# Retention heads of a FoX/RetNet trunk: the second head's p2 product moved up to p1 and p5, and a PSUM bank for each half of the first head's queries and keys

## Chip, cores and metric

The kernel runs on one core of one Trainium2 chip. The metric is the device time of one execution in microseconds (us), lower is better; the time shown is the median of three runs.

## The reference, cut to what matters

Two layers on a sequence of 512 rows of width 2048, all in float32: a forgetting-attention layer, then a chunkwise retention layer with 8 heads. The change lies in the retention layer, whose projections and heads are these:

```
proj = jnp.einsum('bsd,de->bse', x, w_in)
q, k, v, gate = jnp.split(proj, [...], axis=-1)
q = rotary(q.reshape(B, S, RET_HEADS, RET_QK_DIM))
k = rotary(k.reshape(B, S, RET_HEADS, RET_QK_DIM)) * (RET_QK_DIM ** -0.5)
...
inner = jnp.einsum('bhqd,bhkd->bhqk', qc, kc) * intra_decay[None]
...
o = group_norm_heads(o).reshape(B, S, RET_V_WIDTH)
y = o * jax.nn.silu(gate)
return jnp.einsum('bse,ed->bsd', y, w_out)
```

A head's queries and keys are 256 columns each, its values and gates 512 each.

## The kernel before, in words

**Products.** Every projection is a matrix product of 2x2 quarters. A `Unit` does it in Strassen's way with seven products p1 to p7 of sums of quarters; a `Plain` unit does the eight plain products. Each float32 operand is split into a high and a low part (`split`: ScalarE writes the high part w_h, L305, then VectorE subtracts to the low part w_l, L306), and each product is three matmuls (L310, L311, L312). A product is cut into blocks along the contraction: a wide unit (values and gates, 512 columns) has four blocks a product with 12 matmuls of 512 columns each, a narrow unit (queries and keys) two with 24 of 256. A `Unit` adds into three accumulators, x, y and z, each a tile of two PSUM banks (the kernel calls such a tile a bank, and so does this text; tags b0, b1, b2, kept in the list `banks`). p1, p6, p7 and p4 add into x, p2 into y, p5 and p3 into z. When a product ends whose sum is needed later, ScalarE copies its accumulator to SBUF (`keep`, L423) into a buffer with one of the tags k0, k1, k2, y0.

**Order of blocks.** `ORDER` lists the products in groups whose blocks alternate: p1 with p5 (one block later), then p6, then p3 with p7, then p2 with p4. A pair in `SHARES` (p2 before p4) that stands side by side shares one loaded quarter of the weights. Buffers for loaded quarters are few: three tags and a fourth, `room`; chains of sums sit in four w_q buffers; there are three pairs of w_h and w_l.

**Retention layer.** Head 0's queries and keys are a `Plain` unit run in two halves, `EACH[0]` (rows m = 0) and `EACH[1]` (m = 1). Between the halves head 0's wide unit does p2 and p1 (`FIRST`), and after them p5, p6, p3, p7 and p4 (`REST`). Both halves of queries and keys use one bank, `banks[0]`; ScalarE copies a half out of it (`take_qk`, L1576, tile qk_raw). `REST`'s p5 then uses that same bank as its z. Heads 1 to 7 each do a narrow unit and then a wide unit in `ORDER`.

**What else runs.** A planner (`Order`) writes the program: it places a block of matmuls a slot, and between blocks the steps of tasks, as far as rings of buffers are free and the work handed to VectorE and ScalarE stays under a limit. If a block or a `keep` needs a buffer that is not free, `require` places steps of waiting tasks one after another, with no block between them, until it is. Two tasks run beside a head's wide unit. `attend` does the rotary embedding of the head's own queries and keys on VectorE (tile rope, L1609 to L1616), splits them (qk_h, qk_l), and does four scores (mmp<-qk_h), a mask (L1659) and a split (inner). `retain` ends the head before: bn_stats, a Newton inverse root in small VectorE steps (L289 to L301, L1733), four times a scaling on ScalarE (L1753), a transpose on TensorE (L1740), two copies (y L1744, ny L1745), and stores issued on POOL. At its third step `retain` gives back the buffer k0 (first gate half), which the wide unit's p1 is to be kept in. Head 1's p5 is kept in y0, the other heads' in k1.

Of the kernel before, what the change touches and what calls it, by code (L numbers as in the profile page):

```python
# [23 lines left out]
RH = 8  # L24
# [28 lines left out]
FIRST = (("p2",), ("p1",))  # L53
REST = (("p5",), ("p6",), ("p3", "p7"), ("p4",))
ORDER = (("p1", "+p5"), ("p6",), ("p3", "p7"), ("p2", "p4"))

EARLY = (("p1",), ("p5",), ("p2", "p6"), ("p3",), ("p7",), ("p4",))

# [29 lines left out]
class Order:  # L88
# [29 lines left out]
    def spawn(self, steps, rank=2):  # L118

        task = dict(steps=steps, last=self.now - 1, rank=rank)  # L120
        try:
            task["need"] = next(steps)
        except StopIteration:
            return
        at = sum(t["rank"] <= rank for t in self.tasks)
        self.tasks.insert(at, task)
# [104 lines left out]
def trunk(ctx: ExitStack, tc: tile.TileContext, xq, x, fb_f, columns, wf_in, narrow, wide, ln_g, ln_b, rot, decay,  # L231
# [94 lines left out]
    banks = ["b0", "b1", "b2"]  # L326
# [37 lines left out]
    class Unit:  # L364
# [3 lines left out]
        def __init__(self, w, n, sink, rows=True, u2="k0", p1="k0"):  # L368
            self.w, self.n, self.sink, self.rows, self.u2, self.p1 = w, n, sink, rows, u2, p1
            self.wide = w is wide  # L370
            self.shape = [P, 2, 512] if self.wide else [P, 4, 256]
            self.blocks = 8 // self.shape[1]
            self.tags = None
            self.early = self.between = self.adds = False
            self.p15_tag = self.p5 = "k1"
            self.bank, self.kept, self.chain, self.lent, self.summed = {}, {}, {}, {}, {}
            self.left = {p: self.blocks for p in FORM}
            self.kept_w, self.of = {}, {}
# [115 lines left out]

        def run(self, order=ORDER, then={}, leaves=False, last=False):


            self.early = order is EARLY
            self.leaves, self.last = leaves, last
            order = blocks_of(self.blocks, *order)  # L500

            i = order.index(("p3", self.blocks - 1)) if ("p3", 0) in order else 0
            if order[i + 1:i + 3] == [("p7", self.blocks - 1), ("p4", 0)]:
                order[i:i + 2] = order[i + 1], order[i]
            for i, (p, c) in enumerate(order):
                shares = i + 1 < len(order) and order[i + 1] == (SHARES.get(p), c)
                shared = i > 0 and order[i - 1] == ({"p7": "p3", "p4": "p2"}.get(p), c)
                turned = p == "p7" and order[i + 1] == ("p3", c) or p == "p3" and order[i - 1] == ("p7", c)
                e = (0,) if last and p == "p4" else (0, 1)
                o.push(Block(self, p, c, e, shares, shared, then.get(i), then.get(p), turned))  # L510
            for c in range(4 if last else 0):
                o.push(Block(self, "p4", c, (1,), False, False, None, None))
# [362 lines left out]
    def fetch_while(i):  # L875

        take = lambda *names: lambda: spawn(fetch_forms(i, names))
        return {"p5": take("a11"), "p6": take("s1"), "p7": take("s2", "s4"), "p4": take("s3", "a12", "a22")}
# [632 lines left out]
    def biases():  # L1511

        nc.gpsimd.dma_start(row_b, ln_b[1:2, :])
        for s in range(8):
            yield need(wait=12)
            nc.gpsimd.dma_start(out[s * 64:(s + 1) * 64, :], row_b[0:1, :].to_broadcast([64, D]))
# [23 lines left out]
    class Head:  # L1540
        def __init__(self, h):
            self.h = h
            self.raw = self.v = None
            self.ends = [], []
            self.have = self.have_v = self.have_g = 0
            self.gates = {}
            self.attended = False
            if h == 0:
                self.qk_unit = Plain(narrow, 8, self.take_qk, lambda: [banks[0]] * 2, rows=False)
            else:  # L1550
                self.qk_unit = Unit(narrow, 8 + h, self.take_qk, rows=False, u2="y0")
                if h == 1:

                    self.qk_unit.u2, self.qk_unit.p15_tag = "k1", "y0"
            self.vg_unit = Unit(wide, 6 + h, self.take_vg, u2="k2")
            if h == 1:
                self.vg_unit.p5 = "y0"

        def take_qk(self, m, n, tile, done):

# [223 lines left out]
    for h in heads[1:]:  # L1784
        if h.h == 2:
            spawn(biases())
        h.qk_unit.run(then={"p3": lambda h=h: spawn(h.attend())})
        then = fetch_while(1) if h.h == RH - 1 else {}
        last = then.get("p4", lambda: None)
        h.vg_unit.run(leaves=h.h == RH - 1,  # L1790
                      then={**then, "p4": lambda h=h, last=last: (spawn(h.retain()), last())})


# [141 lines left out]
```

## Time and profile before

| | before |
|---|---|
| median of 3 runs | 2405.23 us (2400.59 to 2405.72) |
| the profiled execution | 2403.45 us |
| its span, first to last instruction | 2401.7 us |
| mean granted TensorE clock | 0.988 |
| TensorE matmuls (PE), busy share | 97% |
| VectorE (DVE) | 79% |
| ScalarE (ACT) | 51% |
| POOL | 7% |

The profiled execution's time is its span and 1.75 us around it. PE is TensorE's matmuls, PEld its weight loads, DVE VectorE, ACT ScalarE, SP the queue that issues most loads. Times in views are microseconds from the span's start. An idle time in brackets stands with what ended it.

### The profile page before, as it was taken

What the parts mean: (1) busy time and instruction counts of PE and PEld (TensorE: products, weight loads), DVE (VectorE), ACT (ScalarE), POOL (GpSimd) and SP (SyncE); (2) the same over time, 40 slices, a digit from 0 to 9 for tenths busy, and PEclk for the clock granted to TensorE, in tenths of its full rate; (3) what the DMA queues carried; (4) which work ended last, traced back from release to release, by engine and by line L of the source; (5) the groups of instructions that cost most, each with busy time, mean ns of one, the idle gap of its engine ahead of it and who ended that gap; (6) DMA issues with size and microseconds to landing.
All of it is one profiled execution on the core that took longest, in us unless ns stands there. A gap on an engine that the chain in (4) does not pass through costs nothing.

```text
span 2401.7 us, 34231 instructions
## 1 busy us (share of the span) xinstructions
PE 2320.4 (97%) x13096; PEld 2014.9 (84%) x13096; DVE 1894.4 (79%) x2483; ACT 1216.2 (51%) x1774; POOL 160.7 (7%) x248
## 2 busy tenths in 40 slices
PE   9999999999999999989899999999999999999995
PEld 9888798798799778878779898888889898777784
DVE  5888778678765656679878888898888889987977
ACT  4556556556555534555354545454544445544533
POOL 0000000000000000010020101010101001011002
PEclk9999999999999999999999999999999999999998
DMA  6355544554544467675575857675665659689778
GB/s 225 123 199 175 164 162 159 175 180 153 185 150 156 134 205 233 221 174 154 175 219 194 246 183 220 206 195 187 209 199 193 210 172 265 211 268 292 242 244 190
DMA packets 184564, 471.16 MB, mean 196 GB/s; under 512 B 17968, under 2 KB 63168, under 8 KB 183888
## 3 DMA queue, kind: packets, MB, share of 16 engines
q1 hardware_dynamic: 159136, 395.29, 49.9%
q0 software_dynamic: 25264, 73.69, 12.2%
q8 instruction: 103, 1.69, 0.3%
q14 instruction: 61, 0.50, 0.1%
HBM read 411.20 MB, written 61.91 MB: 197 GB/s over the span
## 4 chain that ended last, share of the span: by engine, by line
PE 44%; DVE 5%; DMA 3%; issue 2%; ACT 1%; POOL 0%; ACTq 0%; DVEq 0%; POOLq 0%
PE acc L310 13%; PE acc L311 13%; PE acc L312 13%; DVE w_l L306 2%; DMA w_raw<-in_wide 2%; PE mmp L310 1%; PE mmp L311 1%; PE mmp L312 1%; DVE w_q L575 1%; ACT w_h L305 1%; PE mmp L1740 0%; DVE z L1840 0%; DMA y_s<-ny 0%; DMA y_s<-y 0%; DMA z_half<-z_in 0%
## 5 line engine op out<-in xcount | busy, mean ns | idle before, releaser
L305 ACT ACTIVATE w_h<-w_q 128x1024 fp32r<-128x1024 f32 x360 | 380.4, 1059 | 425.5 <-DVE w_q L575 218.3
L310 PE MATMUL acc<-w_h,a 128*128 128x512 f32 (+1 forms) x1536 | 551.4, 359 | 6.2 <-DVE kept L468 3.5
L311 PE MATMUL acc<-w_l,a 128*128 128x512 f32 (+1 forms) x1536 | 545.3, 355 | 1.8 <-DVE w_l L306 1.8
L306 DVE TENSOR_TENSOR w_l<-w_raw,w_h 128x1024 fp32r<-128x1024 f32 x314 | 383.4, 1222 | 206.2 <-ACT w_h L305 205.3
L312 PE MATMUL acc<-w_h,a 128*128 128x512 f32 (+1 forms) x1536 | 545.1, 355 | 0.0
L306 DVE TENSOR_TENSOR w_l<-w_q,w_h 128x1024 fp32r<-128x1024 f32 x360 | 439.3, 1221 | 118.1 <-ACT w_h L305 111.1
L310 PE MATMUL acc<-w_h,s 128*128 128x512 f32 (+1 forms) x1408 | 515.9, 366 | 4.3 <-ACT qk_raw L1576 2.1
L311 PE MATMUL acc<-w_l,s 128*128 128x512 f32 (+1 forms) x1408 | 512.0, 364 | 8.0 <-DVE w_l L306 7.9
L312 PE MATMUL acc<-w_h,s 128*128 128x512 f32 (+1 forms) x1408 | 510.1, 362 | 0.0
L305 ACT ACTIVATE w_h<-w_raw 128x1024 fp32r<-128x1024 f32 x314 | 331.7, 1058 | 346.7 <-PE acc L312 161.5
L310 PEld LDWEIGHTS acc<-w_h,a 128*128 128x128 f32 x1536 | 290.9, 189 | 48.3 <-issue 7.4
L311 PEld LDWEIGHTS acc<-w_l,a 128*128 128x128 f32 x1536 | 291.0, 189 | 42.5 <-DVE w_l L306 4.8
L312 PEld LDWEIGHTS acc<-w_h,a 128*128 128x128 f32 x1536 | 290.8, 189 | 41.2
L311 PEld LDWEIGHTS acc<-w_l,s 128*128 128x128 f32 x1408 | 267.6, 190 | 51.4 <-DVE w_l L306 13.6
L310 PEld LDWEIGHTS acc<-w_h,s 128*128 128x128 f32 x1408 | 267.5, 190 | 44.1 <-ACT w_h L305 3.0
L312 PEld LDWEIGHTS acc<-w_h,s 128*128 128x128 f32 x1408 | 267.4, 190 | 41.2
L575 DVE TENSOR_TENSOR w_q<-w_q,w_raw 128x1024 f32<-128x1024 f32 x216 | 263.2, 1220 | 9.0 <-DMA w_raw<-in_wide 6.5
L310 PE MATMUL acc<-a,w_h 128*128 128x256 f32 x464 | 132.9, 287 | 4.3 <-ACT qk_raw L1576 3.1
L312 PE MATMUL acc<-a,w_l 128*128 128x256 f32 x464 | 132.7, 286 | 0.8 <-DVE w_l L306 0.8
L311 PE MATMUL acc<-a,w_h 128*128 128x256 f32 x464 | 132.5, 286 | 0.0
L312 PE MATMUL acc<-s,w_l 128*128 128x256 f32 x448 | 126.8, 283 | 0.0
L311 PE MATMUL acc<-s,w_h 128*128 128x256 f32 x448 | 126.7, 283 | 0.0
(231 smaller groups left out, 2976.3 us busy)
## 6 DMA issues: line engine op xcount, KB each, us to landing
w_raw<-in_wide SPq DMA_DIRECT2D x321, 512.0 KB, 4.0
w_raw<-in_narrow SPq DMA_DIRECT2D x144, 512.0 KB, 3.7
w_q<-in_wide SPq DMA_DIRECT2D x64, 512.0 KB, 4.6
room<-in_wide SPq DMA_DIRECT2D x47, 512.0 KB, 5.0
w_q<-in_narrow SPq DMA_DIRECT2D x26, 512.0 KB, 4.0
y_s<-ny POOLq DMA_DIRECT2D x48, 256.0 KB, 7.0
y_s<-y POOLq DMA_DIRECT2D x40, 256.0 KB, 5.9
room<-in_narrow SPq DMA_DIRECT2D x18, 512.0 KB, 4.5
```

The costliest lines, as they stand in the source:

```text
L305: nc.scalar.activation(h, src, AF.Copy)
L306: nc.vector.tensor_sub(l, src, f32(h))
L310: nc.tensor.matmul(ps, a[0], b[0], start=start, stop=False, skip_group_check=True)
L311: nc.tensor.matmul(ps, a[0], b[1], start=False, stop=False, skip_group_check=True)
L312: nc.tensor.matmul(ps, a[1], b[0], start=False, stop=stop, skip_group_check=True)
L575: nc.vector.tensor_add(u.chain[c], u.chain[c], t)
```

## The change

A new order `SLOW` has p2 alternate with p1 and p5, and p4 alone at the end. Head 1's wide unit uses it, and keeps p5 in k1, as other heads do, instead of y0. Head 0's `Plain` unit takes `banks[0]` for its first half and `banks[2]` for its second; the list is read when the first half begins.

```diff
+SLOW = (("p1", "p2", "+p5"), ("p6",), ("p3", "p7"), ("p4",))
...
             if h == 0:
-                self.qk_unit = Plain(narrow, 8, self.take_qk, lambda: [banks[0]] * 2, rows=False)
+                self.qk_unit = Plain(narrow, 8, self.take_qk, lambda: [banks[0], banks[2]], rows=False)
...
             self.vg_unit = Unit(wide, 6 + h, self.take_vg, u2="k2")
-            if h == 1:
-                self.vg_unit.p5 = "y0"
...
         h.qk_unit.run(then={"p3": lambda h=h: spawn(h.attend())})
...
-        h.vg_unit.run(leaves=h.h == RH - 1,
+        h.vg_unit.run(SLOW if h.h == 1 else ORDER, leaves=h.h == RH - 1,
```

`banks[2]` at that moment is the tag that `FIRST` then takes as p2's y, and p2 is copied out of it when p1 begins. With p2 away from p4 the two no longer share a quarter: head 1's p4 loads its own, four loads of 512 KB more on SP (848 rows there, 844 before).

**Place 1: TensorE, from the last matmuls of the first head's `EACH[1]` to the first of its p5** (acc_9849 is the bank of the second half, s1 the operand of p5; what an instruction waits for stands in brackets). Before:

```order
L310 MATMUL acc_9849<-a22_9795,w_h_10008 128x256
L311 MATMUL acc_9849<-a22_9796,w_h_10008 128x256
L312 MATMUL acc_9849<-a22_9795,w_l_10009 128x256
L310 MATMUL acc_10109<-w_h_10038,s1_9876 128x512 [waits PE_49,Activation_49]
L311 MATMUL acc_10109<-w_l_10039,s1_9876 128x512 [waits DVE_49]
L312 MATMUL acc_10109<-w_h_10038,s1_9877 128x512
```

Now, at the same place (line numbers from 57 to 1555 are two higher in the changed file):

```order
L312 MATMUL acc_9849<-a22_9795,w_h_10008 128x256
L313 MATMUL acc_9849<-a22_9796,w_h_10008 128x256
L314 MATMUL acc_9849<-a22_9795,w_l_10009 128x256
L312 MATMUL acc_10106<-w_h_10038,s1_9876 128x512 [waits Activation_49]
L313 MATMUL acc_10106<-w_l_10039,s1_9876 128x512 [waits DVE_49]
L314 MATMUL acc_10106<-w_h_10038,s1_9877 128x512
```

No instruction moved; the accumulator of p5 is another, and its first matmul now waits for ScalarE alone (for which of its instructions, the view does not tell).

**Place 2: TensorE, the first transposes of head 0's `retain` inside head 1's wide unit** (a is an operand of p1 or p2, s one of p5). Before:

```order
L310 MATMUL acc<-w_h,a_9028 128x512
L311 MATMUL acc<-w_l,a_9028 128x512
L312 MATMUL acc<-w_h,a_9029 128x512
L1740 MATMUL mmp<-ident,kept 128x128 x8
L310 MATMUL mmp<-qk_h 128x512
L311 MATMUL mmp<-qk_l,qk_h 128x512
L312 MATMUL mmp<-qk_h,qk_l 128x512
```

Now:

```order
L312 MATMUL acc<-w_h,a_9030 128x512
L313 MATMUL acc<-w_l,a_9030 128x512
L314 MATMUL acc<-w_h,a_9031 128x512
L1740 MATMUL mmp<-ident,kept 128x128 x4
L312 MATMUL acc<-w_h,s_9876 128x512
L313 MATMUL acc<-w_l,s_9876 128x512
L314 MATMUL acc<-w_h,s_9877 128x512
```

Before, two transposes and the first score stood in a row behind the seventh block, with p5's last block behind them; now a whole block of 12 matmuls stands between any two of these steps, and the first score stands behind all twelve blocks of p1, p2 and p5.

**Place 3: ScalarE in the same stretch, from the copy out of head 1's narrow unit (L1576) on** (w_q are weights of p1 or p5, w_raw and room those of p2). Before:

```order
L1576 ACTIVATE kept<-acc 128x512
L305 ACTIVATE w_h<-w_q 128x1024 x6
L1753 ACTIVATE kept<-kept,gn_r 128x512
L305 ACTIVATE qk_h<-rope 128x2x2x256
L1753 ACTIVATE kept<-kept,gn_r 128x512
L305 ACTIVATE qk_h<-rope 128x2x2x256
L1744 ACTIVATE y<-mmp 128x512
L1745 ACTIVATE ny<-mmp 128x512
L1753 ACTIVATE gate<-gate,gn_r 128x512
L423 ACTIVATE kept<-acc 128x1024
L305 ACTIVATE w_h<-w_q 128x1024
```

Now:

```order
L1753 ACTIVATE kept<-kept,gn_r 128x512
L307 ACTIVATE w_h<-w_raw 128x1024
L1744 ACTIVATE y<-mmp 128x512
L1745 ACTIVATE ny<-mmp 128x512
L1753 ACTIVATE gate<-gate,gn_r 128x512
L307 ACTIVATE qk_h<-rope 128x2x2x256
L307 ACTIVATE w_h<-w_q 128x1024 x2
L1744 ACTIVATE y<-mmp 128x512
L1745 ACTIVATE ny<-mmp 128x512
L1753 ACTIVATE gate<-gate,gn_r 128x512
L307 ACTIVATE w_h<-room 128x1024
```

Before, eight ScalarE steps of the two tasks and the copy of p1 stood between the splits of two blocks; now the splits lie among them.

## Rows read from the trace of the kernel before

**Rows 1.** The page's part 1: busy time, share of the span and instructions.

```profile
PE 2320.4 (97%) x13096; PEld 2014.9 (84%) x13096; DVE 1894.4 (79%) x2483; ACT 1216.2 (51%) x1774; POOL 160.7 (7%) x248
```

**Rows 2.** Stretches: us, busy PE, PEld, DVE, ACT, POOL, PEclk, DMA share, GB/s.

```profile
1062.82:1108.21 45.39, 45.39 (x193) 37.27 (x194) 38.30 (x37) 22.38 (x22) 5.26 (x6) 0.96 0.61 133
1170.07:1269.96 99.89, 85.63 (x379) 70.27 (x377) 76.15 (x99) 45.39 (x53) 12.46 (x19) 0.91 0.61 183
1317.14:1399.56 82.42, 82.36 (x379) 68.17 (x377) 71.47 (x72) 44.27 (x52) 12.34 (x19) 1.00 0.74 228
```

**Rows 3.** PE in order of time, 1188.8 to 1207.8: start, us, [idle before].

```profile
1188.69 0.39 PE L311 MATMUL acc<-w_l,a 128*128 128x512 f32 x1
1188.91 0.39 PE L312 MATMUL acc<-w_h,a 128*128 128x512 f32 x1
1191.06 0.65 PE L1740 MATMUL mmp<-ident,kept 128*128 128x128 f32 x4 [1.76 <-ACT kept L1753]
1196.83 1.12 PE L1740 MATMUL mmp<-ident,kept 128*128 128x128 f32 x4 [5.12 <-ACT kept L1753]
1204.72 0.79 PE L310 MATMUL mmp<-qk_h 128*128 128x512 f32 x1 [6.78 <-ACT ny L1745]
1205.32 0.63 PE L311 MATMUL mmp<-qk_l,qk_h 128*128 128x512 f32 x1
1205.74 0.63 PE L312 MATMUL mmp<-qk_h,qk_l 128*128 128x512 f32 x1
```

**Rows 4.** ACT in order of time, 1187 to 1206.

```profile
1195.11 1.06 ACT L305 ACTIVATE qk_h<-rope 128x1024 fp32r<-128x1024 f32 x1 [4.10 <-DVE rope L1616]
...
1201.12 1.06 ACT L305 ACTIVATE qk_h<-rope 128x1024 fp32r<-128x1024 f32 x1 [4.35 <-DVE rope L1616]
```

**Rows 5.** PE in order of time: three matmuls that had waited.

```profile
862.31 0.47 PE L310 MATMUL acc<-w_h,a 128*128 128x512 f32 x1 [1.70 <-DVE z L1412]
...
1036.20 0.58 PE L310 MATMUL acc<-a,w_h 128*128 128x256 f32 x1 [3.11 <-ACT qk_raw L1576]
...
1062.82 0.67 PE L310 MATMUL acc<-w_h,s 128*128 128x512 f32 x1 [2.05 <-ACT qk_raw L1576]
```

**Rows 6.** Stretches behind such waits, columns as in rows 2.

```profile
862.00:866.00 4.00, 3.69 (x16) 3.11 (x17) 1.98 (x3) 0.69 (x1) 0.00 (x0) 1.00 0.68 206
...
1036.20:1039.10 2.90, 2.89 (x13) 2.90 (x14) 2.90 (x3) 1.50 (x2) 0.00 (x0) 0.50 0.76 243
...
1062.99:1066.41 3.42, 3.42 (x9) 2.65 (x10) 1.20 (x2) 0.00 (x0) 0.87 (x1) 0.50 0.97 171
...
1192.70:1209.77 17.07, 6.16 (x16) 4.69 (x17) 12.35 (x20) 6.27 (x8) 2.16 (x4) 0.50 0.54 162
```

**Rows 7.** ACT and DVE in order of time around 1033.

```profile
1032.24 1.05 ACT L305 ACTIVATE w_h<-w_raw 128x1024 fp32r<-128x1024 f32 x1
...
1035.08 1.07 ACT L1576 ACTIVATE qk_raw<-acc 128x512 f32<-128x512 f32 x2
...
1033.52 1.22 DVE L306 TENSOR_TENSOR w_l<-w_raw,w_h 128x1024 fp32r<-128x1024 f32 x1
1034.66 1.22 DVE L306 TENSOR_TENSOR a<-raw,a 128x1024 fp32r<-128x1024 f32 x1
```

**Rows 8.** DVE in order of time: rows that price its steps.

```profile
1160.73 1.23 DVE L306 TENSOR_TENSOR w_l<-w_q,w_h 128x1024 fp32r<-128x1024 f32 x1
...
1193.15 0.15 DVE L299 TENSOR_TENSOR rsq_t<-gn_r 128x2 f32<-128x2 f32 x1
1193.34 0.16 DVE L300 TENSOR_TENSOR rsq_t<-rsq_t,rsq_h 128x2 f32<-128x2 f32 x1
...
1199.20 0.68 DVE L1613 TENSOR_TENSOR rope<-kept,sin 128x512 f32<-128x512 f32 x1
```

**Rows 9.** DMA issues from 1170.07 to 1269.96: count, KB, median us to landing.

```profile
w_raw<-in_wide SPq DMA_DIRECT2D x11, 512.0 KB, 4.9
```

**Rows 10.** Waits of ACT, 1120 to 1320: us in total, times, longest.

```profile
ACT y L1744 <- DMA y_s<-y: 1.1, 1, 1.1
```

## The prediction

> **What bounds the kernel now.** I read the page's busy shares first: matmuls are busy for 97% of the span and VectorE for 79% [rows 1], so time is to be had only where TensorE stands still or runs at its lower clock. Then I set stretches side by side. A wide unit of 379 matmul records takes 82.42 us in head 2 and 99.89 us in head 1 [rows 2], so head 1's loses 99.89 - 82.42 = 17.5 us to something that head 2's lacks. The order of time on TensorE shows where: between the seventh block's last matmul at 1188.91 and the first score lie three waits of 1.76, 5.12 and 6.78 us, 13.7 in all [rows 3], and the granted clock is 0.50 from 1192.70 to 1209.77 [rows 6], so that the score's matmuls start 0.42 us apart instead of 0.22 [rows 3]. ScalarE holds these steps up: its two scalings and the copies stand in order behind two splits of rope, which waited 4.10 and 4.35 us for VectorE [rows 4]. The stall is thus one serial chain of VectorE and ScalarE that the program placed between two blocks, with no matmuls to cover it. Head 0 has two more: its second half of queries and keys waited 3.11 us, and its p5 2.05 us, both for ScalarE's copy out of the one bank that they share [rows 5]. [...]
>
> **First head's banks.** No instruction is added or moved; two matmuls lose a wait.
>
> The second half starts in another bank. Its first matmul then needs w_h, ready at 1032.24 + 1.05 = 1033.29, but the third needs w_l, which VectorE starts only at 1033.52 and ends at 1034.74 [rows 7]. TensorE comes free at about 1033.1 (1036.20 - 3.11), does two short matmuls (2.89 us over 13 of them at half clock [rows 6], so 0.11 at full clock), and waits for w_l: 1034.74 - 1033.1 - 0.22, some 1.4 us, are still lost. What is late next is therefore VectorE, and of the 3.11 us I take back 1.7. The lower clock cost half of 2.90, 1.45 us [rows 6]. Whether it falls again after 1.4 us I take from the nearest row: after a wait of 1.70 us at 862.31 [rows 5] the clock stayed at 1.00 [rows 6]. So 1.7 + 1.45 = 3.15; the ends are 1.45 (the clock falls all the same, and 1.7 is lost again, half of 3.42) and 4.55 (no wait at all).
>
> p5 takes a bank whose content was copied out at 1035.08 [rows 7], 27 us ahead. Its weights were split before the wait ended, since VectorE and ScalarE keep two blocks ahead. So all of 2.05 goes, and with it half of 3.42: 2.05 + 1.71 = 3.76. The rest of the stretch to 1108.21 is matmuls without a gap [rows 2] and moves up as it is. Together 3.15 + 3.76 = 6.9 us; ends 5.2 and 8.3.
>
> **Second head's order.** *What goes.* p1's last block is now the tenth of the unit, not the seventh, so k0 is asked for three blocks later, when the two tasks have reached that point by themselves. The transposes, the rotary steps and the score are placed with whole blocks between them. If none waits, the unit takes head 2's 82.42 us, for it has the same matmuls: 17.5 us back. This contains the lower clock after 1192.70.
>
> *What VectorE must do.* This is the cover, and it is thin. From the end of the first block's w_l at 1161.96 [rows 8] to the start of the twelfth block, its list now holds 11 w_l, 5 sums of weights, 2 rope products and 1 qk_l, 19 of 1024 columns at 1.14 us from start to start (1033.52 to 1034.66) [rows 7]: 21.7. With 9 steps of 512 columns at 0.68 [rows 8], 6.1; two groups of bn_stats with their product, estimated at two and a half such steps each, 3.4; 26 small steps at 0.19 [rows 8], 4.9. In all 36 us. TensorE gives it from 1161.96 to about 1202: the unit's start 1170.07 [rows 2], eleven blocks of 12 x 0.2275 = 2.73 us (the pitch of 0.22 to 0.23 of rows 3) and four transposes of some 0.4. That is 40 us, and buffers for w_h and w_l let VectorE be only about two blocks ahead, so by estimate it loses some 2 us at the start. Going through the list block by block with these prices, each w_l is ready before its block; the least spare time is under 1 us, at the eighth and eleventh blocks. I take 1 us off: 16.5. The ends: all of 17.5, or 11.5, if two blocks wait about 2 us each and the clock falls once (1.7).
>
> *ScalarE.* The second y must wait until the first y's stores have let go of its buffer. Now two splits of weights stand between them, in place of four. The longest such wait in this stretch was 1.1 us [rows 10], less than the two blocks that ScalarE is ahead.
>
> *Loads.* Four more of 512 KB on SP, for p4, at 4.9 us each from issue to landing [rows 9]. They stand behind residual loads that wait for stores, but a buffer comes free each block and the DMA share in the stretch was 0.61 [rows 2]. I cost them at nothing; matmuls of p3 and p7, eight blocks or 22 us, cover them. If a load came late with that cover gone, its 4.9 us less a block's 2.73 would show, four times, 8.7 at most; the lower end of 11.5 holds about half of that.
>
> *Keeps.* p1, p2 and p5 are copied or added as before, each once; y0 is replaced by k1, which the second rope half frees before p5's last block. p2's accumulator is needed already in the second block, 2.75 us after the unit's start, and the copy that frees it (L1576) ran at once after the last narrow block, so it costs nothing. What follows head 1 keeps its order of instructions.
>
> **Sum.** 6.9 + 16.5 = 23.4 us. Against the profiled execution: 2403.45 - 23.4 = 2380.0. That execution lies 1.8 us under the median of the three runs; half of this added gives my forecast, **2381 us**, for the median.
>
> **Rivals.**
>
> *VectorE becomes the bound in head 1's first twelve blocks.* For: 36 us of work in 40, with hand-overs of rope to ScalarE and back on top. Against: VectorE was busy for 76 of 99.9 us [rows 2], and in the same stretch no matmul waited before the two tasks' steps stood in its way. Waits of 4 to 8 us and one or two falls of the clock would leave 8 to 11 us of the 17.5: 2403.45 - 6.9 - 8 to 11 gives 2385.5 to 2388.5, up to 2391 with the scatter of the runs. Chance 0.13.
>
> *The stall returns at another place* (ScalarE behind the y stores, or SP's loads of p4), and only a few us of it are gained: 2403.45 - 6.9 - 0 to 5 = 2391.5 to 2396.5. Chance 0.05. In its weak form only the banks fail, because TensorE was waiting for w_l as well; then their first term falls to 1.45 and the time is about 2382, inside the range.
>
> *Both parts do nothing* that can be measured: the bank's wait is replaced by w_l's, and the chain keeps its length. Then about 2403. Chance 0.03. Against: the waits name the copy, and the order shows the chain broken up.
>
> [...] Chance 0.02. [...]
>
> **How the numbers follow.** The forecast, both stalls mostly gone, has 0.77. The terms' ends give 2403.45 less 16.7 to 25.8, so 2377.7 to 2386.8. The three runs lie from 2.9 below to 2.3 above the profiled time; with this 2375 to 2389, and on to 2391 for the first rival. About 5 us, 0.2%, is what a measurement of this kernel can tell from no change: faster by more than that 0.95, within it 0.03, slower 0.02.
>
> **What would show it.** Right: matmuls after 1033 begin about 1.4 us after the last ones and wait for w_l, not for qk_raw; no wait before p5; the stretch from head 1's first wide block to head 2's first narrow one takes 82.5 to 84 us at a clock near 1.00, with the transposes waiting under 0.5 us. Wrong: waits of over 1 us for w_l within the twelve blocks, a wait of ScalarE's y for stores of over 3 us, a clock of 0.5 anywhere between, or p4's matmuls behind sums that wait for their loads.

## The result and the profile after

| | before | after |
|---|---|---|
| median, runs side by side | 2405.02 us (2400.59 to 2405.72, 4 runs) | 2381.93 us (2379.64 to 2383.73, 4 runs) |
| the profiled execution | 2403.45 us | 2381.27 us |
| its span | 2401.7 us | 2379.4 us |
| mean granted TensorE clock | 0.988 | 0.994 |

The ratio is 0.9907, with an interval of 0.9890 to 0.9925. The medians lie 23.1 us apart and the profiled executions 22.2, where 23.4 were forecast; the median is 2381.93 us, where 2381 was forecast.

The profile's page for the changed kernel, part 1 (busy time, share of the span, instructions), against [rows 1]:

```profile
PE 2314.7 (97%) x13096; PEld 2009.6 (84%) x13096; DVE 1893.0 (80%) x2483; ACT 1216.2 (51%) x1774; POOL 161.0 (7%) x248
```

The shares say nothing of the gain: they hardly move. It must be read from stretches. I cut both executions at the first matmul of each unit (narrow is queries and keys, wide is values and gates):

| stretch | before | after | gained |
|---|---|---|---|
| start to head 0's `EACH[0]` | 978.67 | 979.29 | -0.62 |
| `EACH[0]` | 26.86 | 25.86 | 1.00 |
| `FIRST`, to the first matmul of `EACH[1]` | 30.67 | 28.43 | 2.24 |
| `EACH[1]`, to the first matmul of p5 | 26.62 | 24.35 | 2.27 |
| `REST` | 57.60 | 55.88 | 1.72 |
| head 1, narrow | 49.65 | 49.66 | -0.01 |
| head 1, wide | 99.89 | 83.27 | 16.62 |
| head 2's narrow unit to the end | 1131.7 | 1132.7 | -0.9 |

Of the stretches in [rows 2], the same three after the change (us, busy PE, PEld, DVE, ACT, POOL, PEclk, DMA share, GB/s; the first is all of `REST` here):

```profile
1057.93:1113.81 55.88, 55.88 (x248) 46.11 (x247) 50.87 (x49) 30.68 (x31) 6.12 (x7) 1.00 0.72 179
1163.47:1246.74 83.27, 82.67 (x378) 68.11 (x377) 74.65 (x99) 44.11 (x53) 11.86 (x18) 1.00 0.77 239
1293.92:1376.35 82.43, 82.37 (x379) 68.18 (x378) 71.39 (x72) 44.28 (x52) 12.35 (x19) 1.00 0.74 228
```

Head 1's wide unit now takes head 2's time and 0.84 us more, at a granted clock of 1.00. VectorE has done the same 75 to 76 us of work in 16.6 us less.

**The first head's banks.** TensorE in order of time, where `EACH[1]` and p5 begin (start, us, engine, line, [idle before and what ended it]); these answer to [rows 5]. Then VectorE's step that makes the low part for the first block of `EACH[1]`, to set against [rows 7]:

```profile
1033.58 0.39 PE L312 MATMUL acc<-a,w_h 128*128 128x256 f32 x1 [0.25 <-ACT w_h L307]
1033.80 0.28 PE L313 MATMUL acc<-a,w_h 128*128 128x256 f32 x1
1035.03 0.39 PE L314 MATMUL acc<-a,w_l 128*128 128x256 f32 x1 [0.94 <-DVE w_l L308]
...
1057.93 0.40 PE L312 MATMUL acc<-w_h,s 128*128 128x512 f32 x1
```

```profile
1033.75 1.22 DVE L308 TENSOR_TENSOR w_l<-w_raw,w_h 128x1024 fp32r<-128x1024 f32 x1
```

The waits of 3.11 and 2.05 us for qk_raw are gone. 0.25 for w_h and 0.94 for w_l have come in the place of the first, nothing in the place of the second, and the granted clock stays at 1.00 behind both (1033.58 to 1057.93).

**The second head's steps.** The transposes of head 0's `retain` and the first score in head 1's wide unit, against [rows 3] (matmuls into the accumulators left out):

```profile
1180.31 0.60 PE L1740 MATMUL mmp<-ident,kept 128*128 128x128 f32 x4
...
1186.25 0.60 PE L1740 MATMUL mmp<-ident,gate 128*128 128x128 f32 x4
...
1198.08 0.39 PE L312 MATMUL mmp<-qk_h 128*128 128x512 f32 x1
```

None has an idle time before it, where 1.76, 5.12 and 6.78 us stood. In the whole unit TensorE waits 0.6 us, for w_l.

**VectorE's cover.** Two stretches: that of the prediction's account, from the end of the first block's w_l to the start of the twelfth block, and that of the twelve blocks of p1, p2 and p5 (the twelfth ends where the first score begins, at 1198.08). Then the low parts of the third, the eighth and the eleventh block as VectorE makes them, and the first matmul that reads the last two:

```profile
1155.36:1195.36 40.00, 40.00 (x207) 33.96 (x206) 35.92 (x62) 22.06 (x28) 7.56 (x12) 1.00 0.57 176
1163.47:1198.08 34.61, 34.61 (x162) 28.60 (x161) 32.60 (x55) 22.48 (x28) 8.13 (x13) 1.00 0.67 206
```

```profile
1164.69 1.23 DVE L308 TENSOR_TENSOR w_l<-w_q,w_h 128x1024 fp32r<-128x1024 f32 x1 [2.07 <-ACT w_h L307]
...
1180.96 1.22 DVE L308 TENSOR_TENSOR w_l<-w_raw,w_h 128x1024 fp32r<-128x1024 f32 x1
...
1190.18 1.22 DVE L308 TENSOR_TENSOR w_l<-room,w_h 128x1024 fp32r<-128x1024 f32 x1
```

```profile
1183.75 0.39 PE L313 MATMUL acc<-w_l,a 128*128 128x512 f32 x1
...
1192.87 0.39 PE L313 MATMUL acc<-w_l,a 128*128 128x512 f32 x1
```

VectorE is busy for 35.9 of the 40 us of the account, and for 32.6 of 34.6 us of the twelve blocks, while TensorE never stops. The eighth w_l is ready at 1182.18 and read at 1183.75, the eleventh at 1191.40 and 1192.87: 1.57 and 1.47 us to spare, the least of the blocks from the second to the twelfth. The change works with one and a half microseconds in hand.

**The four extra loads.** VectorE and TensorE at p4, and the two kinds of loads in the unit (count, KB, median us to landing; [rows 9] for w_raw before):

```profile
1235.58 1.23 DVE L577 TENSOR_TENSOR w_q<-w_q,room 128x1024 f32<-128x1024 f32 x1 [1.39 <-DMA room<-in_wide]
```

```profile
1241.39 0.50 PE L313 MATMUL acc<-w_l,a 128*128 128x512 f32 x1 [0.39 <-DVE w_l L308]
```

```profile
w_raw<-in_wide SPq DMA_DIRECT2D x13, 512.0 KB, 6.0
room<-in_wide SPq DMA_DIRECT2D x5, 512.0 KB, 7.7
```

Loads land later than before (w_raw 6.0 for 4.9 us). One came 1.39 us late for VectorE, and a little later a matmul waited 0.39 us for a w_l; 0.22 us at 1237.99, in p4 too, is the unit's only other wait. That these follow from the late load is only argued, by the order of VectorE's steps. `p2_early` and `dose4` below have the same four loads and no wait in p4, so 0.6 us is the most that the loads cost here.

### The profile page after: what moved, and what is told of

Same layout as the page of the kernel before. It is cut to its first block, busy times and chain, and to the rows that moved or that the text cites. A ratio compares the mean times of both kernels' runs of the same rounds, so it can differ in the third digit from the quotient of the medians.

```text
span 2379.4 us, 34242 instructions
## 1 busy us (share of the span) xinstructions
PE 2314.7 (97%) x13096; PEld 2009.6 (84%) x13096; DVE 1893.0 (80%) x2483; ACT 1216.2 (51%) x1774; POOL 161.0 (7%) x248
## 4 chain that ended last, share of the span: by engine, by line
PE 58%; DVE 7%; DMA 4%; issue 3%; ACT 3%; POOL 0%; SPq 0%; ACTq 0%; DVEq 0%; POOLq 0%
PE acc L312 17%; PE acc L314 17%; PE acc L313 17%; DVE w_l L308 3%; ACT w_h L307 2%; DMA w_raw<-in_wide 2%; PE mmp L312 1%; PE mmp L313 1%; PE mmp L314 1%; DVE w_q L577 1%; DMA v_sum<-in_wide 1%; PE mmp L1220 1%; DMA room<-in_wide 1%; PE mmp L1740 1%; DVE z L1840 0%
## 5 line engine op out<-in xcount | busy, mean ns | idle before, releaser
L313 PEld LDWEIGHTS acc<-w_l,s 128*128 128x128 f32 x1408 | 266.8, 190 | 51.4 <-DVE w_l L308 13.7
```

The source lines that it names most:

```text
L313: nc.tensor.matmul(ps, a[0], b[1], start=False, stop=False, skip_group_check=True)
```

## The experiments

All were timed beside the kernel before, whose median was 2404.13 (17 runs), 2402.37 (11) and 2403.0 us (13) in the three sets. "Wide unit" is head 1's.

| run | what differs | median us | ratio [interval] | wide unit us |
|---|---|---|---|---|
| banks_only | before, new banks | 2395.28 | 0.9969 [0.9959, 0.9980] | 100.28 |
| order_only | after, old banks | 2388.11 | 0.9943 [0.9926, 0.9960] | 82.57 |
| p2_early | after, p1 with p2, then p5 | 2381.52 | 0.9919 [0.9903, 0.9935] | 84.23 |
| p1_y0 | banks, old order, p1 kept in y0 | 2405.01 | 1.0006 [0.9996, 1.0015] | 99.34 |
| slow_y0 | after, p5 kept in y0 | 2380.42 | 0.9908 [0.9891, 0.9925] | 83.02 |
| order_k1 | after, old order | 2395.56 | 0.9973 [0.9963, 0.9983] | 100.19 |
| dose4 | after, 4 more VectorE steps | 2381.66 | 0.9912 [0.9898, 0.9927] | 85.07 |
| dose12 | after, 12 more VectorE steps | 2391.38 | 0.9952 [0.9937, 0.9967] | 93.87 |
| loose_limit | order_k1, planner's limit raised | 2385.33 | 0.9928 [0.9913, 0.9943] | 87.41 |
| tight_p2e | p2_early, planner's limit lowered | 2403.68 | 1.0003 [0.9993, 1.0013] | 106.58 |
| loose_after | after, planner's limit raised | 2386.46 | 0.9930 [0.9915, 0.9945] | 88.42 |

### One part alone

The banks in the kernel before:

```diff
-                self.qk_unit = Plain(narrow, 8, self.take_qk, lambda: [banks[0]] * 2, rows=False)
+                self.qk_unit = Plain(narrow, 8, self.take_qk, lambda: [banks[0], banks[2]], rows=False)
```

> The first head's banks alone, the second head in the old order. Theory (two separate stalls, each with its own cause): only the head-0 part of the gain, 5 to 7 us, so about 2398 to 2400 beside 2405 for the kernel before; the second half's first wait is for w_l (about 1 us), there is none before p5, the second head's wide unit still takes 99.9 us. Rival (the parts feed each other: starting 6 us earlier alone lets head 0's end be done before the seventh block): the wide unit falls below 95 us and the time below 2394.

The medians differ by 2404.13 - 2395.28 = 8.9 us, more than the 5 to 7 of the theory; the interval of the ratio reaches from 4.8 to 9.9 us. The waits for qk_raw are gone, w_l's of 0.94 us is there, and `EACH[0]` to the end of `REST` takes 134.4 us in place of 141.8, 7.4 less. Of this 0.57 lies in `FIRST`, ahead of the new bank: its transposes wait for ScalarE's raw for 0.29 us here and 0.86 in the kernel before, a wait that differs from one execution to the next (last section). That leaves 6.8 us. The wide unit stays as it was, 100.28 us at a granted clock of 0.91, so the rival is out.

The same line put back in the changed kernel:

> The second head's order and p5 in k1 alone, the first head's halves in one bank. Theory: the second head's wide unit takes 83.3 us as in the changed kernel, the waits of 3.1 and 2.1 us for qk_raw stay, 2405 - 16.6 = 2388.5. Rival (the parts feed each other): the unit takes over 86 us, the time is over 2391.

TensorE at the two places, and the stretches behind:

```profile
1038.47 0.58 PE L312 MATMUL acc<-a,w_h 128*128 128x256 f32 x1 [3.13 <-ACT qk_raw L1576]
```

```profile
1065.27 0.50 PE L312 MATMUL acc<-w_h,s 128*128 128x512 f32 x1 [2.05 <-ACT qk_raw L1576]
```

```profile
1038.47:1041.37 2.90, 2.90 (x13) 2.90 (x14) 2.90 (x3) 1.50 (x2) 0.00 (x0) 0.50 0.74 260
1065.27:1068.69 3.42, 3.42 (x9) 2.70 (x10) 1.37 (x2) 0.00 (x0) 0.87 (x1) 0.56 1.04 180
1172.56:1255.13 82.57, 82.40 (x378) 68.09 (x377) 74.61 (x99) 44.07 (x53) 11.82 (x18) 1.00 0.75 240
```

With the old bank both waits return, to within 0.02 us of [rows 5], with the low clock behind them, and the wide unit does without its stall, as the theory had it. Within the scatter the two parts of the change add up: 2404.13 - 2388.11 = 16.0 us for the order and 8.9 for the banks make 24.9, against 23.1 for both in their own set.

### The buffer that p5 is kept in

The change moved p5 from y0 to k1. Back to y0, all else as changed:

```diff
             self.vg_unit = Unit(wide, 6 + h, self.take_vg, u2="k2")
+            if h == 1:
+                self.vg_unit.p5 = "y0"
```

> The changed kernel with one part undone: head 1's p5 is kept in y0 again instead of k1. TensorE's order of instructions is the changed kernel's. Theory (the gain comes from where the two tasks' steps stand among the blocks; the buffer that p5 is kept in is incidental): head 1's wide unit 82.5 to 84 us, head 2's narrow unit 47.2, time 2381 to 2383. Rival (k1 instead of y0 is part of the gain, because y0 comes free late): head 1's wide unit 85 us or more with a wait at p5's keep, or head 2's narrow unit longer than 48; time 2385 or more.

And new banks and k1, with the old order:

```diff
-        h.vg_unit.run(SLOW if h.h == 1 else ORDER, leaves=h.h == RH - 1,
+        h.vg_unit.run(ORDER, leaves=h.h == RH - 1,
```

> The changed kernel with the old order for head 1, so that new banks and p5 in k1 are left. TensorE's order of instructions in head 1's wide unit is the one before. Theory (the order alone makes the 16.6 us of head 1): head 1's wide unit 99 to 101 us with three waits of about 1.8, 5 and 7 us, time 2394 to 2398, as with the banks alone. Rival (k1 frees something early enough to matter under the old order too): head 1's wide unit under 95 us, time under 2391.

The wide unit of the first, then of the second:

```profile
1161.92:1244.94 83.02, 82.60 (x378) 68.11 (x377) 74.64 (x99) 44.17 (x53) 11.85 (x18) 1.00 0.76 238
```

```profile
1162.79:1262.98 100.19, 85.92 (x378) 70.48 (x377) 76.17 (x99) 45.39 (x53) 12.43 (x19) 0.91 0.60 183
```

In the second, the three waits of [rows 3] stand again, of 1.76, 5.12 and 6.78 us. In the first, head 2's narrow unit takes 47.18 us, as in the changed kernel. The buffer does nothing; of the two, the order of blocks alone decides between 83 and 100 us.

### Is it that the copy of p1 comes later?

The prediction reasoned that k0 is asked for three blocks later, when the tasks have reached that point by themselves. Here p1's copy stands at the seventh block again, as before; its neighbours are blocks of p2 in place of p5:

```diff
-SLOW = (("p1", "p2", "+p5"), ("p6",), ("p3", "p7"), ("p4",))
+SLOW = (("p1", "p2"), ("p5",), ("p6",), ("p3", "p7"), ("p4",))
```

> As the changed kernel, but p2 alternates with p1 alone and p5 comes behind both: p1's last block is the seventh again, as before the change, and its keep asks for k0 there. Theory 1 (the keep was too early; what helps is that it comes later): the stall is back, the wide unit takes 95 to 100 us, 2393 to 2399. Theory 2 (VectorE's load per block decides: p1 and p2 blocks have one VectorE step each and p5's two, so the tail of head 0 gets on earlier where no sums are): the unit takes 82.5 to 86 us and the time is 2380 to 2385, although the keep is no later than before.

The wide unit, and its only wait on TensorE:

```profile
1161.93:1246.16 84.23, 82.85 (x378) 68.02 (x377) 74.57 (x99) 44.72 (x54) 12.37 (x19) 1.00 0.73 226
```

```profile
1197.46 0.33 PE L1740 MATMUL mmp<-ident,gate 128*128 128x128 f32 x1 [1.23 <-ACT ny L1745]
```

So the later copy is not needed: theory 2 held. In the order of instructions the transposes stand between whole blocks here too. A block of p5 asks VectorE for two steps of 1024 columns, a sum of weights and a w_l, one of p2 for w_l alone. The planner places a step of a task only while what it has handed to VectorE stays under 4.4; next to p2 it finds that room ahead of the copy, next to p5 it does not, and `require` then puts the steps in a row. This reason is read from the planner's text; the runs on its limit, below, test it.

The other way round: the old order, with nothing asked of k0, because p1 is kept in y0:

```diff
-            self.vg_unit = Unit(wide, 6 + h, self.take_vg, u2="k2")
-            if h == 1:
-                self.vg_unit.p5 = "y0"
+            self.vg_unit = Unit(wide, 6 + h, self.take_vg, u2="k2", p1="y0" if h == 1 else "k0")
```

(with the new banks)

> Old order of blocks, new banks, p5 in k1, and p1 kept in y0 instead of k0, so that the seventh block's keep no longer needs the buffer that head 0's tail holds. Theory 1 (only k0 at the seventh block was missing): no wait over 1 us in p1 and p5; the unit takes 83 to 86 us, 2381 to 2385. Theory 2 (the tail itself is late, and the next keep that needs one of its buffers will wait: p6's, in k2): the wait moves to the end of p6, 8 to 17 us long, the unit takes 91 to 100 us, 2390 to 2399.

Head 1's wide and head 2's narrow unit, a stretch of the latter, and the wait in it:

```profile
1163.36:1262.70 99.34, 88.56 (x378) 71.23 (x377) 76.23 (x99) 45.48 (x53) 12.43 (x19) 0.95 0.61 184
1262.70:1319.39 56.69, 51.70 (x383) 50.12 (x382) 42.23 (x69) 24.22 (x32) 11.50 (x18) 0.94 0.64 205
1290.90:1297.70 6.80, 5.71 (x27) 5.71 (x28) 4.63 (x17) 4.46 (x7) 2.18 (x4) 0.50 0.35 127
```

```profile
1291.99 0.48 PE L1740 MATMUL mmp<-ident,room 128*128 128x128 f32 x1 [5.00 <-ACT room L1753]
```

The row of steps is gone from the seventh block, and nothing is won: nine waits of 0.4 to 2.8 us spread over the wide unit, and head 2's narrow unit takes 56.7 instead of 47.2 us. The gain of the banks is eaten up, too. Neither theory held: the waits did not go, and they did not move to the end of p6 in one piece; 2405.01 us is worse than both forecast. The tasks seem only to fall behind to the next place that asks for a buffer, but what forces the later steps was not followed further.

### The planner's limit, both ways

If the row of steps is the cause, the old order should lose its stall when the planner may hand out more, and `p2_early` should get one when it may hand out less. First the old order (new banks, p5 in k1) with the limits of 4.4 and 3.8 raised in the blocks of p1 and p5:

```diff
+        if b.u.wide and b.u.n == 7 and b.p in ("p1", "p5"):
+            self.most = 9.0, 9.0
         self.step()
```

> Head 1's wide unit in the old order of blocks (p1 with p5, p1's copy asked for at the seventh block), with the new banks and p5 in k1; only the planner's limit on the work handed to VectorE and ScalarE is raised from 4.4 and 3.8 to 9 in the blocks of p1 and p5. Head 0's transposes then stand between whole blocks. Theory A (what cost 16.6 us was the row of steps that the limit left over for the copy; VectorE has the spare time): head 1's wide unit 82.5 to 85 us, time 2380 to 2384. Theory B (the old order asks more of VectorE in its first seven blocks than it has, so the planner's limit was right and p2's light blocks are needed): waits for w_l of 3 to 8 us in all with falls of the clock, unit 87 to 95, time 2386 to 2394.

The stretches of the wide unit and of 3.5 us behind its first wait; then that wait on TensorE, and VectorE ahead of it (lines are two higher still in this file and the next):

```profile
1163.89:1251.30 87.41, 84.27 (x378) 69.28 (x377) 75.42 (x99) 45.00 (x53) 12.33 (x19) 0.98 0.67 209
1174.80:1178.30 3.50, 3.50 (x11) 2.85 (x12) 3.26 (x8) 0.00 (x0) 0.00 (x0) 0.71 0.02 5
```

```profile
1174.77 0.50 PE L315 MATMUL acc<-w_l,s 128*128 128x512 f32 x1 [2.31 <-DVE w_l L310]
```

```profile
1167.52 0.16 DVE L293 TENSOR_SCALAR rsq_h<-gn_mv 128x2 f32<-128x2 f32 x1
...
1169.96 1.22 DVE L1611 TENSOR_TENSOR rope<-room,cos 128x1024 f32<-128x1024 f32 x1
...
1172.30 1.29 DVE L1618 TENSOR_TENSOR rope<-rope 128x512 f32<-128x512 f32 x2
1173.50 1.22 DVE L310 TENSOR_TENSOR w_l<-w_q,w_h 128x1024 fp32r<-128x1024 f32 x1
```

100.19 - 87.41 = 12.8 us come back without any change of the order of blocks. The unit's time is in theory B's range, at its lower end; the time of 2385.33 us lies between the two forecasts, and the wait for w_l is under B's 3 to 8 us. The steps now stand among the blocks, but in one lump: 13 small ones and a half of the rotary steps, 1167.52 to 1173.50, 6 us of VectorE ahead of one w_l, which TensorE then waits for, with a fall of the clock to 0.71 behind it. The limit of 4.4 keeps such a lump from forming. Of the 4.4 us that are left to the 83.0 of `slow_y0`, this wait and one of 0.83 us (VectorE's kept) are 3.1, and the low clock behind the first is 1.0 (0.29 of 3.5). Whether a limit between 4.4 and 9 would leave less was not tried, so what p2's light blocks are worth beyond the placing stays open.

Then `p2_early` with VectorE's limit lowered:

```diff
+        if b.u.wide and b.u.n == 7 and b.p in ("p1", "p2"):
+            self.most = 2.0, LIMIT[1]
         self.step()
```

> The run with p1 beside p2 alone, its copy at the seventh block, which took 84.2 us in head 1's wide unit, and now the planner's limit for VectorE lowered from 4.4 to 2.0 in those eight blocks. The blocks and their loads are the same; three steps of the two tasks stand in a row behind the seventh block again. Theory (a row of steps without a block between them makes the stall, whatever the order of blocks): waits of 8 to 15 us behind the seventh block, the clock at 0.5 behind them, unit 94 to 102, time 2391 to 2399. Rival (p2's light blocks give VectorE the time to run ahead, and the row costs little): unit under 88, time under 2386.

Its wide unit and the stretch of the stall, then TensorE's waits in it:

```profile
1163.63:1270.21 106.58, 86.63 (x378) 69.70 (x377) 75.85 (x99) 44.16 (x53) 11.83 (x18) 0.92 0.58 180
1184.00:1208.00 24.00, 11.06 (x40) 8.63 (x41) 17.97 (x38) 8.11 (x11) 2.17 (x4) 0.64 0.32 112
```

```profile
1190.16 1.12 PE L1742 MATMUL mmp<-ident,kept 128*128 128x128 f32 x4 [7.30 <-ACT kept L1755]
1197.30 1.11 PE L1742 MATMUL mmp<-ident,kept 128*128 128x128 f32 x4 [6.02 <-ACT kept L1755]
1199.17 0.80 PE L314 MATMUL mmp<-qk_h 128*128 128x512 f32 x1 [0.76 <-ACT ny L1747]
```

The blocks and loads are those of `p2_early`, and so are the numbers of instructions on each engine; only the place of the steps is another. 22.4 us are lost, more than expected: 14.1 us of waits behind the seventh block and 5.9 in six waits after it, less the 1.2 that `p2_early` had; the rest, 3.6 us, goes with the low clock (0.92 over the unit, with TensorE busy for 86.63 us; 1.00 and 82.85 in `p2_early`). Together with `loose_limit` this shows the cause: a row of steps of one serial chain, with no block of matmuls between them.

### How thin is VectorE's cover?

In the changed kernel the subtraction for the low part is done twice, in p2's four blocks, and then in all twelve:

```diff
+            if u.wide and u.n == 7 and p in ('p2',):
+                nc.vector.tensor_sub(self.w[1], raw, f32(self.w[0]))
```

> The changed kernel with VectorE's subtraction for the low part of the weights done twice in the four p2 blocks of head 1's wide unit: 4 more steps of 1.14 us, 4.6 us of VectorE's time within the first eight blocks. The prediction's account (VectorE has 36 us of work in 40, least spare under 1 us): waits for w_l of 1 to 3 us in all, unit 84.5 to 87, time 2383 to 2386. Rival (the account was too tight, VectorE's real spare is over 4.6 us): unit 83 to 84, time within 1 us of the changed kernel's.

The two waits of TensorE over 0.3 us (L605 is the second subtraction):

```profile
1184.17 0.50 PE L313 MATMUL acc<-w_l,a 128*128 128x512 f32 x1 [0.89 <-DVE w_l L605]
...
1194.65 0.50 PE L313 MATMUL acc<-w_l,a 128*128 128x512 f32 x1 [1.07 <-DVE w_l L605]
```

They stand at the eighth and the eleventh block, where the cover was least. The unit takes 85.07 us, 2.05 more than in `slow_y0` of the same set: of 4.6 us added, 2.6 were hidden. Unit and waits are as the account had them. The time, 2381.66 us, is under its 2383 to 2386 and where the rival put it; an interval of 0.9898 to 0.9927, some 7 us wide, cannot tell 2 us, so the unit decides.

> The same with the subtraction done twice in all twelve blocks of p1, p2 and p5 of head 1's wide unit: 12 more steps, 13.7 us of VectorE's time. The prediction's account (spare 2 to 4 us in all): 10 to 12 us of waits for w_l or the steps behind it, plus 1 to 6 us if the clock falls; unit 93 to 101, time 2391 to 2399. Rival (VectorE's real spare is about 8 us or more): unit under 90, time under 2388.

The waits of TensorE in the unit, and the stretches behind the last two:

```profile
PE acc L313 <- DVE w_l L605: 6.7, 4, 2.3
```

```profile
1188.70:1192.20 3.50, 3.48 (x9) 2.77 (x10) 3.47 (x4) 1.28 (x3) 2.15 (x4) 0.55 0.76 262
...
1201.70:1205.20 3.50, 3.48 (x9) 2.79 (x10) 3.47 (x4) 2.61 (x4) 0.41 (x1) 0.56 1.01 335
```

Waits of 1.59, 0.63, 2.32 and 2.15 us, 6.7 in all, and two falls of the clock behind the last two, about 1.6 us each (0.45 of 3.5): 9.9 of the 10.85 us by which the unit is longer than `slow_y0`'s. Of 13.7 us added, 7 were hidden. So the total spare lies between the account's 2 to 4 us and the rival's 8, and the waits (10 to 12 were expected) were too dear by 3 us or more. Unit and time fell into the account's range at its lower end, with the help of the clock's 3.1 us.

Last, the changed kernel with the limits raised to 9 in the twelve blocks, so that scores stand among them:

> The changed kernel with the limit raised to 9 for head 1's twelve blocks of p1, p2 and p5, so that scores stand among them too. If VectorE's spare in the changed kernel is about 2.6 us, as the doubled subtractions suggest, a score's mask and split (some 2 to 3 us of VectorE for the first two) would just fit: unit 82.5 to 84, time within 2 us of the changed kernel's. Rival (VectorE is the bound once scores are among them): waits for w_l of 2 us or more, unit 85 or more.

```profile
PE acc L315 <- DVE w_l L310: 3.4, 4, 1.5
PE mmp L314 <- ACT ny L1747: 1.4, 1, 1.4
```

88.42 us, 5 more than the changed kernel: four waits for w_l and one for ny. The rival held: there is no room for a score's mask and split where the spare was 1.5 us. For the new order a limit of 4.4 is better than one of 9; nothing between them was tried. No version tried beats the changed kernel by more than the scatter (`slow_y0` has 2380.42 in another set, at the same ratio).

## Why the prediction was right, step by step

**What bounds the kernel.** Right: TensorE's busy share stayed at 97% and VectorE's went from 79% to 80%, while the gain lay in two stretches with idle time and a low clock (0.50 behind their waits, [rows 6]).

**The first head's banks, 6.9 us.** p5: the wait of 2.05 went and `REST` lost 1.72 us of low clock (0.50 for 3.42 us before, [rows 6]; 1.00 over all of `REST` now), 3.77 for a forecast of 3.76. The second half: from the moment that TensorE came free to p5's first matmul it took 29.73 us before (1033.09 to 1062.82), 27.68 without p5's wait, and 24.60 now (1033.33 to 1057.93): 3.08 less, for a forecast of 3.15. The step "1.4 us are still lost" was right: VectorE ended w_l at 1034.97, 1.64 us after TensorE came free, as in the kernel before. The two waits show 1.19 us of this; the rest is the two matmuls between them, shown as 0.51 us. That the clock would stay up behind this wait was taken from a single row, and did come out so in the changed kernel: 1.00 from 1033.58 to 1057.93. Together 6.85, and 6.8 in `banks_only`.

**The second head's order, 16.5 us.** 16.62. The forecast of 17.5 less 1 for waits was right in size, but the last microsecond by luck: it was taken off for waits in the twelve blocks, and there was none. The 0.84 us over head 2's time are 0.6 us of waits for w_l, both in p4, which had been costed at nothing, and 0.2 spread.

**VectorE's account, 36 us in 40, least spare under 1 us at the eighth and the eleventh block.** The places were right, and so was the sum: VectorE was busy for 35.9 of the same 40 us, with a wait of 2.07 us for w_h at the start (some 2 were estimated). 1.57 and 1.47 us were to spare: under 1 was a little too dark. Small steps weigh in the chain: a step of two columns took 0.16 us where one of 1024 took 1.22 ([rows 8]; the same in `loose_limit`), and the 13 small steps of a Newton root took 2.4 us (1167.52 to 1169.96 in `loose_limit`), as long as two steps of 1024 columns.

**Why the stall goes.** Here the number was right and the reason was not the one that counts. The prediction said: k0 is asked for three blocks later, when the tasks have reached that point by themselves. `p2_early` has the copy at the old place and gains 15.7 of the 16.6 us in the unit. What counts is that the steps can be placed between blocks ahead of the copy, and p2's blocks, which ask less of VectorE, leave the planner that room. `loose_limit` and `tight_p2e` show the placing to be the cause, from both sides.

**ScalarE's second y.** No wait of y for its stores is left in the unit (1.1 us before, [rows 10]); right.

**The loads, nothing.** 0.6 us at p4 at most, and none in `p2_early`. Loads landed later (w_raw 6.0 for 4.9 us, room 7.7 for 4.5), and p4 has the unit's only waits for w_l, of 0.22 and 0.39 us.

**The rivals.** VectorE as the bound: not in the changed kernel, but `dose12` shows how near it was; 13.7 us more of its work cost 10.9. A stall at another place: not here, though `p1_y0` shows that way of failing at full price. Both parts doing nothing: no. A slower kernel, at 0.02: no. That chance was the author's estimate, and no run shows a ground for it. The twelve blocks go round x, y and z with a new bank each block; the clock was granted 1.00 over all of them, 1163.47 to 1198.08, and TensorE was busy for all of these 34.61 us.

**What balanced.** The span lost 22.3 us, against terms of 6.85 + 16.62 = 23.5. The start ran 0.6 us longer in this execution and the stretch from head 2 on 0.9. `EACH[0]` ran 1.0 shorter, and `FIRST` 0.6 longer up to TensorE's coming free; these two belong together (last section). None of this was forecast.

## What to carry to other kernels

Where a planner or a hand-written order must run the steps of a side task at once to free a buffer, look at the chain inside that row: each step waits for another engine, TensorE has no matmuls to cover it, and the lost time is the chain's length and the low clock behind it (13.7 us of waits and about 3 us of clock here). Putting blocks that ask little of the side task's engine ahead of the place that asks cured it here; moving the buffer won nothing, and raising the limit on that engine won 12.8 us where the order of blocks won 17. Then read the spare time that is left, block by block, and test it with a doubled step: here 1.5 us at the least, and the next 4.6 us of work on VectorE already showed, with 2 us.

## What the runs showed of the hardware that was not expected

The same two waits, 1.2 and 0.75 us, stand 1.3 us apart at the start of `EACH[0]` in every execution. Behind them the clock fell in some and not in others. The kernel before and the changed kernel, in the 3.41 us that begin 1.15 us behind the second wait's end:

```profile
981.08:984.49 3.41, 3.41 (x18) 3.41 (x17) 3.41 (x5) 0.57 (x1) 0.00 (x0) 0.50 0.51 165
```

```profile
981.70:985.11 3.41, 3.41 (x29) 3.28 (x28) 3.41 (x5) 1.06 (x1) 0.00 (x0) 1.00 0.49 160
```

`EACH[0]` took 26.8 to 26.9 us in the seven of the thirteen profiled executions in which the clock fell there (0.50 to 0.68 over these 3.4 us), and 25.9 to 26.0 in the other six (1.00); both kinds are found with the old banks and the new, and with either order. So a term of about 1 us of clock in one stretch can be chance. It did not reach the total either: `EACH[0]` and `FIRST` together took 54.1 to 54.6 us in ten of the eleven executions with the new banks (55.2 in `loose_limit`), whether the clock fell or not. Where it stayed up, `FIRST`'s transposes waited 1.2 us or more for ScalarE's raw in these executions (1.23 in the changed kernel); where it fell, 0.3 to 0.8 us (0.29 in `banks_only`). What sets the pace of raw was not followed.

A single wait of about 2 us did not tell by its length whether the clock would fall behind it. It stayed at 1.00 behind 0.94 (the changed kernel), 1.23 (`p2_early`), 1.59 (`dose12`) and 1.70 us ([rows 5]). It fell behind 2.05 ([rows 5]; 0.50 over 3.42 us), 2.15 and 2.32 (`dose12`; 0.56 and 0.55 over 3.5) and 2.31 us (`loose_limit`; 0.71 over 3.5), and behind 1.86 us at 2195.98 in the kernel before (0.53 over 3.5). But it stayed at 1.00 behind 2.05 us at 2196.39 in `tight_p2e`, 2.42 us at 2183.52 in `dose12`, and 2.62 us in head 1's wide unit of `tight_p2e`, which is this wait and the stretch behind it:

```profile
1251.27 0.50 PE L315 MATMUL acc<-w_l,s 128*128 128x512 f32 x1 [2.62 <-DVE w_l L310]
```

```profile
1251.27:1254.77 3.50, 3.50 (x15) 2.92 (x16) 3.50 (x5) 1.93 (x4) 0.00 (x0) 1.00 0.88 224
```

The 1.7 us of clock that the prediction took with p5's wait was there in both executions with the old bank (0.50 and 0.56 over 3.42 us, so 1.7 and 1.5); at another place a wait of the same length cost no clock.
